# Second head's key weights loaded ahead of the pool's, and token block 2 turned ahead of the value projection, in a two-layer decoder trunk

## The chip, the cores and the metric

The kernel runs on one core of a Trainium2 chip. The metric is the device time of one execution in microseconds (us). The kernel before was timed three times: 1939.69, 1940.29 and 1944.26 us, so its median is 1940.29 us. One more execution was taken with the hardware profiler: it took 1946.18 us in all, of which the traced span, from the first to the last instruction, is 1944.4 us. "Line" numbers such as L276 are lines of the kernel before.

## What is computed

A decoder trunk of two layers over 512 tokens of width 1024, in float32. Cut to its frame, the reference is

```python
for i in range(DEPTH):                     # DEPTH = 2, a = (2 * DEPTH) ** 0.25
    x = layer_norm(a * x + 0.5 * swiglu_ffn(x, ffn_w_in[i, 0], ffn_w_out[i, 0]), ...)
    if m == 0:                             # layer 0
        h = diff_attention(x, da_w_qkv[j], da_w_o[j], da_lam_q[j], da_lam_k[j], ...)
    elif m == 1:                           # layer 1
        h = pool_mixer(x, pool_w[j], pool_b[j], pool_scale[j])
    x = layer_norm(a * x + h, ...)
    x = layer_norm(a * x + memory_cross_attention(x, mem, xa_wq[i], xa_wkv[i], xa_wo[i]), ...)
    x = layer_norm(a * x + 0.5 * swiglu_ffn(x, ffn_w_in[i, 1], ffn_w_out[i, 1]), ...)
```

Two places matter here. In `diff_attention` the rows of x are projected to values, queries and keys, and two softmaxes of each head are combined with a scalar lambda, which is computed from `da_lam_q` and `da_lam_k` (products, sums, two exponentials). In `pool_mixer` x is averaged over four causal windows, a small matrix per group of columns is applied, and a bias and a scale follow. The cross attention behind it needs keys and values of 256 memory rows, `mem @ xa_wkv`, for four heads; they don't depend on x.

## The kernel before, in words

**Numbers.** Every float32 operand of a matmul is split into a high part, which ScalarE (ACT) writes as a rounded copy, and a low part, which VectorE (DVE) writes as the difference (`split`, L116 to L121). A product is three matmuls, high by high, high by low and low by high (`mm3`, L200 to L207). So each block of weights costs one ACT copy and one DVE subtraction before TensorE (PE) can use it.

**Layout.** The 512 tokens are four blocks of 128 rows, `self.X[0]` to `self.X[3]`, which stay in SBUF. For a projection the rows have to lie across: `turn` (L460 to L471) transposes eight 128 by 128 squares of one block on PE into two banks of PSUM and splits them into `xh` and `xl`. `self.late` lists the blocks that are normalised and not yet turned, and `turn_late(wait)` (L448) turns all of them from position `wait` on. `self.turned` holds the last pair of split instructions.

**Order.** Each engine works through its own list of instructions strictly in order. The lists are made at compile time: a scheduler takes the instructions by their place in the program and by when its own model finds them ready, so an instruction that is ready early may be listed ahead of one that stands earlier in the program. `tc.issue_after(i)` lists what is traced in its block behind `i` if both are on one engine; it adds no wait for `i` to finish and no instruction. DMAs of weights are issued from SyncE's queue (SP), in order as well: one that waits for its buffer holds back all behind it. `weave` (L209) interleaves two generators, one that feeds PE steadily and one at its side, by a fixed budget of nanoseconds.

**Where layer 0's attention begins.** The first FFN ends with the layer norm of the four blocks (`summed`, L440, `ln_token`, L363); blocks 0 and 1 are turned while it still runs (L443, L444), blocks 2 and 3 are left in `self.late`. `diff_attention` (L1180) first calls `lam` (L988): two small loads, a product and a sum on DVE, an exponential on ACT, two tiny steps on DVE. Then `da_main` (L1130) projects the values of the first two heads (`da_values`, L1004): blocks 0 and 1 first, then `turn_late()` turns blocks 2 and 3, then blocks 2 and 3. Queries and keys follow head by head. Their weights are split by `cols_rope` (L268 to L277): one ACT copy (L274) and two DVE subtractions (L276).

**Where layer 1's mixer begins.** `mixer` (L1528) traces, in this order: the transposes and splits of the memory rows (`load_memory`), the loads of head 0's key and value weights of the cross attention (`raws`, L1545), the pool's loads (`pool_loads`, L1206: five DMAs, 2 MB, L1211, L1217, L1218), and the splits of x that the pool needs (L1248). Then `weave` runs `early_kv` (L1402), which computes keys and values of heads 0 and 1 through `xa_kv` (L1330), with `pool_mixer` (L1238) at its side. There are two buffers for raw weights of 1 MB, so head 1's key weights can be loaded only when head 0's are split. The pool side has eight steps with band matmuls (L1261 to L1271), each split into `pooled`; behind the second of them stands `pool_weights` (L1221), which scales the pool's matrix and bias on DVE (L1227, L1236). After the eighth the pool's matrix is split, `begin_ln` loads the rows of the norm's gain and bias (`load_row`, L336), and per block two sums (L1282 to L1294) and `ln_token` follow.

Of the kernel before, what the change touches and what calls it, by code (L numbers as in the profile page):

```python
# [9 lines left out]
F32 = mybir.dt.float32  # L10
# [8 lines left out]
D = 1024  # L19
S = 512  # L20
# [79 lines left out]
def drain(units):  # L100
    for _ in units:
        pass
# [7 lines left out]
class Trunk:  # L110
# [74 lines left out]
    def mm(self, name):  # L185
        return self.mmp.tile([P, S], F32, tag="mm", name=name)
# [42 lines left out]

    def raw_cols(self, w, c0, width=256):  # L230
        raw = self.raw_tile((8, 256))
        self.nc.sync.dma_start(
            raw[:, :, :width], w[:, c0 : c0 + width].rearrange("(k p) n -> p k n", p=P)
        )
        return raw
# [29 lines left out]
            self.nc.sync.dma_start(raw[:, j], w[:, c : c + P].rearrange("(k p) n -> p k n", p=P))  # L265
        return raw

    def cols_rope(self, raw, j):  # L268

        nc = self.nc  # L270
        w = self.hl([P, 8, P])
        src = raw[:, j].rearrange("p k (m h q e) -> p (k m) q h e", m=2, h=2, q=2)
        hi, lo = (t.rearrange("p k (m q h e) -> p (k m) q h e", m=2, q=2, h=2) for t in w)
        nc.scalar.copy(hi, src)  # L274
        for q in range(2):
            nc.vector.tensor_sub(lo[:, :, q], src[:, :, q], hi[:, :, q].bitcast(F32))  # L276
        return w  # L277

    def wide(self, raw):
# [198 lines left out]
    def behind(self):  # L478

        return self.tc.issue_after(self.last_mm.ins)  # L480

    def transpose4(self, pt, blocks):
        for j, b in enumerate(blocks):
            self.nc.tensor.transpose(pt[:, j], b, self.ident)
# [645 lines left out]
    def da_main(self):  # L1130

        w, w_o = self.a["da_w_qkv"][0], self.a["da_w_o"][0]
        for n in range(0, DA_H, 2):
            vs = []
            if n < V_FIRST:
                yield from self.da_values(n, vs)
            rq, rk = self.raw_heads(w, n * P), self.raw_heads(w, D + n * P)
            for h in range(n, n + 2):
                q = self.mm("q")
                yield from self.project(q, self.cols_rope(rq, h % 2))  # L1140
                q = self.da_query(q)
                k = self.mm("k")
                yield from self.project(k, self.cols_rope(rk, h % 2))
                k = self.da_key(k)
                sm = self.small("sd", (P, NT, 2))
                self.heads.append((self.clock, {"h": h, "q": q, "k": k, "v": vs, "sm": sm}))
            if not vs:
                yield from self.da_values(n, vs)
        yield from self.to_tokens(self.oT[:4], w_o, 0, 4, True, False, ALPHA)
# [28 lines left out]
                yield W_E[1]  # L1178

    def diff_attention(self, layer, ln):  # L1180
        self.nlam = self.lam()
        self.low_keys = [self.pair("low") for i in range(2)]
        for pair in self.low_keys:
            for m, t in enumerate(pair):
                self.nc.gpsimd.memset(t[HALVES[1 - m]].bitcast(F32), 0.0)
        self.heads, self.oT = [], [None] * DA_H
        self.weave(self.da_main(), self.da_side(), GAP)
        self.begin_ln(layer, ln, 1.0)
        home = lambda tag: lambda: self.pair(tag)
        homes = [[home("qk")] * 4, [home("low"), home("low"), home("p"), home("p")]]  # L1190
        drain(self.to_tokens(self.oT[4:], self.a["da_w_o"][0], 4, 4, False, True, ALPHA, homes))
# [46 lines left out]
    def pool_mixer(self, layer, ln):  # L1238
        nc = self.nc
        bandh, bandf, bandl = self.bandh, self.bandf, self.bandl  # L1240

        self.new_xt()
        xs = [[], []]
        for t in range(NT):
            for half in range(2):
                j = 2 * (t % 2) + half
                x = self.xh[t // 2][:, j], self.xl[t // 2][:, j]
                self.split(x[0], x[1], self.X[t][:, half * S : (half + 1) * S])  # L1248
                xs[half].append(x)
        pooled = []  # L1250
        mm = nc.tensor.matmul
        yield
        for c in range(KC):
            if c == 2:
                with self.tc.issue_after(split[1].ins):
                    self.pool_weights()
            g = c // 2
            half, o = c // 4, slice((c % 4) * P, (c % 4 + 1) * P)
            pp = self.aux("pp")
            with self.behind():  # L1260
                for t in range(NT):  # L1261
                    xh, xl = (x[:, o] for x in xs[half][t])
                    n = BAND if t < NT - 1 else P
                    out = pp[:, t * P : t * P + n]
                    m = (bandf if t == 0 else bandh)[:, g, :n]

                    mm(out, xh, m, start=t == 0, stop=False, skip_group_check=True)
                    if t == 0:
                        m0 = bandl[:, g]
                        mm(out[:, :16], xh, m0, start=False, stop=False, skip_group_check=True)  # L1270
                    mm(out, xl, m, start=False, stop=t == NT - 1, skip_group_check=True)  # L1271
            q = self.pair("pooled")
            split = self.split(q[0], q[1], pp)
            pooled.append(q)
            yield
        wg = self.wide(self.pool_w)
        self.begin_ln(layer, ln, 1.0)
        for t in range(NT):
            o = slice(t * P, (t + 1) * P)
            for half in range(2):  # L1280
                ps = self.aux("ps")
                mm(ps, self.ones, self.pool_b[half], start=True, stop=False)  # L1282
                for j in range(2):
                    g = half * 2 + j
                    for k in range(2):
                        q = pooled[2 * g + k]
                        self.mm3(
                            ps[:, j * 256 : (j + 1) * 256],
                            (q[0][:, o], q[1][:, o]),
                            wg[2 * g + k],  # L1290
                            False,
                            k == 1 and j == 1,
                        )
                self.ln_add(t, half, ALPHA, ps)  # L1294
                yield
            self.turn_late()
            self.ln_token(t)
# [29 lines left out]
        if tag and LINE < 480:  # L1327
            self.stage["mem"].tile([P, (480 - LINE) // 4], F32, name="mempad")

    def xa_kv(self, w, h, raws=None):  # L1330
        nc = self.nc
        rk = raws[0] if raws else self.raw_cols(w, h * 256)
        ps = self.mm("pk").rearrange("p (c n) -> p c n", c=2)
        for j in range(2):
            wk = self.cols(rk, j)
            for k in range(KC):
                yield self.mm3(
                    ps[:, j], (wk[0][:, k], wk[1][:, k]), self.memT[k], k == 0, k == KC - 1
                )
        kv = lambda: tuple(  # L1340
            self.kvp.tile([P, 2, MEM], F32R, tag="kv", name="kv", bufs=8) for _ in range(2)
        )
        kt = kv()
        self.turn_late()
        self.split(kt[0], kt[1], ps)
        wv = self.wide(raws[1] if raws else self.raw_cols(w, D + h * 256))
        ps = self.mm("pv").rearrange("p (m n) -> p m n", m=2)
        for m in range(2):
            o = slice(m * P, (m + 1) * P)
            for k in range(KC):  # L1350
                mt = self.memT[k]
                yield self.mm3(ps[:, m], (mt[0][:, o], mt[1][:, o]), wv[k], k == 0, k == KC - 1)
        v = kv()
        self.split(v[0], v[1], ps)
        return kt, v
# [44 lines left out]
            yield  # L1400

    def early_kv(self, layer, heads, raws):  # L1402
        for h in range(heads):
            self.kv.append((yield from self.xa_kv(self.a["xa_wkv"][layer], h, raws)))
            raws = None

    def xa_main(self, layer):
        wq, wkv = self.a["xa_wq"][layer], self.a["xa_wkv"][layer]
# [119 lines left out]
    def mixer(self, layer, ln):  # L1528
# [5 lines left out]
        else:  # L1534
# [5 lines left out]
            with self.phase_pool(("pooled", "pooled"), "sq", **bufs):  # L1540
                side = self.pool_mixer(layer, ln)
                with self.tc.high_priority():
                    self.load_memory()
                w = self.a["xa_wkv"][layer]
                raws = [self.raw_cols(w, c) for c in (0, D)]  # L1545
                self.pool_loads()
                next(side)
                self.kv = []
                self.weave(self.early_kv(layer, 2, raws), side, 640, 8500)
# [48 lines left out]
```

## Time and profile before

| what | before |
|---|---|
| median of the timed runs | 1940.29 us (1939.69 to 1944.26) |
| profiled execution, in all | 1946.18 us |
| its traced span | 1944.4 us |
| busy: PE / DVE / ACT / GpSimd (POOL) | 99% / 81% / 53% / 15% of the span |
| mean granted clock of PE | 0.994 |
| moved by DMA | 277.96 MB, 143 GB/s on average |

How to read it: PE is busy nearly all the time, so what can be won is PE's idle time, what lies between its matmuls, or time in which PE's clock is not granted in full. The other engines matter where PE waits for one of them. In a timeline a row gives the start, the duration, the engine, the line, the operation, output and inputs, shapes, how many instructions were merged (x4), and in square brackets how long the engine had been idle before and whose end released it. A row of the stretches gives the length, then the busy time of PE, PE's weight loads, DVE, ACT and POOL with the number of instructions, PE's granted clock (1.00 is full), the share of the DMA engines and GB/s.

### The profile page before, as it was taken

The page shows a single profiled execution, that of the slowest core. Times are in us where ns is not written, and L with a number is a line of the kernel's source. Part 1 is how long each engine was busy: PE and PEld are TensorE (multiplying, and loading weights), DVE is VectorE, ACT ScalarE, POOL GpSimd, SP SyncE. Part 2 cuts the span into 40 slices and gives each one's busy share as a digit, 9 for nine tenths or more (in the row PEclk, how much of TensorE's full clock was granted, in tenths as well). Part 3 has the DMA queues.
Part 4 walks back from the last instruction along what each step waited for, and adds up shares of the span by engine and source line. Part 5 has one row for each costly group of instructions (what it writes and reads, how often), then busy time and mean ns, then how long its engine had stood idle before and what let it go on. Part 6 is the DMA issues. An engine that isn't in the chain of part 4 may idle for free.

```text
span 1944.4 us, 32555 instructions
## 1 busy us (share of the span) xinstructions
PE 1916.4 (99%) x13122; PEld 1753.2 (90%) x13122; DVE 1565.4 (81%) x2212; ACT 1025.2 (53%) x1582; POOL 300.3 (15%) x269
## 2 busy tenths in 40 slices
PE   8999999999999999999999999999999999999998
PEld 8999998888778888999998999999898889999997
DVE  7888889888867558889888888898777568988886
ACT  6555454567655435655554655555445336555553
POOL 2112121111110001221220311212000013111210
PEclk9999999999999999999999999999979999999999
DMA  9978772322134317977785687878243347867861
GB/s 240 216 167 181 174 137 77 90 78 75 52 112 141 109 66 194 175 177 163 143 193 170 114 179 163 183 166 173 78 152 131 102 131 134 175 163 170 184 132 60
DMA packets 247031, 277.96 MB, mean 143 GB/s; under 512 B 8288, under 2 KB 212576, under 8 KB 246880
## 3 DMA queue, kind: packets, MB, share of 16 engines
q0 software_dynamic: 92928, 92.29, 30.9%
q1 hardware_dynamic: 153952, 183.59, 28.9%
q8 instruction: 103, 1.69, 0.3%
q14 instruction: 48, 0.39, 0.1%
HBM read 273.75 MB, written 2.10 MB: 142 GB/s over the span
## 4 chain that ended last, share of the span: by engine, by line
PE 80%; DVE 10%; issue 4%; ACT 3%; DMA 2%; POOL 1%; SPq 1%; DVEq 0%; POOLq 0%; ACTq 0%
PE x L204 7%; PE x L205 7%; PE x L206 7%; PE z L205 4%; PE z L204 4%; PE z L206 4%; PE ps L204 3%; PE ps L206 3%; PE ps L205 3%; PE px L204 2%; PE px L206 2%; PE px L205 2%; DVE wl L120 2%; PE y L206 2%; PE x L676 2%
## 5 line engine op out<-in xcount | busy, mean ns | idle before, releaser
L661 POOL DMA_DIRECT2D ra<-in_ffn_w_in_dram x132 | 170.2, 1306 | 1001.0 <-DVE wl L120 966.6
L119 ACT CAST wh<-ra 128x1024 fp32r<-128x1024 f32 x184 | 193.5, 1053 | 218.0 <-PE x L205 72.6
L120 DVE TENSOR_TENSOR wl<-ra,wh 128x1024 fp32r<-128x1024 f32 x184 | 224.0, 1220 | 71.4 <-ACT wh L119 70.8
L119 ACT CAST wh<-rc 128x1024 fp32r<-128x1024 f32 x136 | 143.2, 1053 | 122.0 <-PE x L205 42.0
L204 PE MATMUL x<-xe,wh 128*128 128x256 f32 x704 | 195.5, 278 | 0.0
L205 PE MATMUL x<-xe,wh 128*128 128x256 f32 x704 | 195.3, 277 | 0.0
L206 PE MATMUL x<-xe,wl 128*128 128x256 f32 x704 | 195.2, 277 | 0.0
L119 ACT CAST wh<-b 128x1024 fp32r<-128x1024 f32 x112 | 117.8, 1052 | 134.5 <-PE x L205 68.4
L120 DVE TENSOR_TENSOR wl<-rc,wh 128x1024 fp32r<-128x1024 f32 x136 | 164.7, 1219 | 29.4 <-ACT wh L119 29.0
L120 DVE TENSOR_TENSOR wl<-b,wh 128x1024 fp32r<-128x1024 f32 x112 | 136.7, 1221 | 41.0 <-ACT wh L119 41.0
L204 PE MATMUL x<-xh,wh 128*128 128x256 f32 x544 | 151.4, 278 | 0.0
L205 PE MATMUL x<-xl,wh 128*128 128x256 f32 x544 | 150.9, 277 | 0.0
L206 PE MATMUL x<-xh,wl 128*128 128x256 f32 x544 | 150.9, 277 | 0.0
L205 PEld LDWEIGHTS x<-xe,wh 128*128 128x128 f32 x704 | 132.7, 188 | 1.4
L204 PEld LDWEIGHTS x<-xe,wh 128*128 128x128 f32 x704 | 132.3, 188 | 1.3
L206 PEld LDWEIGHTS x<-xe,wl 128*128 128x128 f32 x704 | 132.2, 188 | 0.0
L120 DVE TENSOR_TENSOR wl<-raw,wh 128x1024 fp32r<-128x1024 f32 x64 | 80.5, 1265 | 56.4 <-ACT wh L119 55.7
L205 PEld LDWEIGHTS x<-xl,wh 128*128 128x128 f32 x544 | 102.6, 189 | 0.7
L204 PEld LDWEIGHTS x<-xh,wh 128*128 128x128 f32 x544 | 102.2, 188 | 0.7
L206 PEld LDWEIGHTS x<-xh,wl 128*128 128x128 f32 x544 | 102.2, 188 | 0.0
L119 ACT CAST wh<-raw 128x1024 fp32r<-128x1024 f32 x64 | 66.5, 1049 | 64.9 <-PE xq L205 21.3
L206 PE MATMUL y<-xh,wl 128*128 128x256 f32 x352 | 98.6, 280 | 1.5 <-DVE wl L120 0.3
(436 smaller groups left out, 6337.1 us busy)
## 6 DMA issues: line engine op xcount, KB each, us to landing
ra<-in_ffn_w_in_dram POOLq DMA_DIRECT2D x132, 512.0 KB, 6.8
rc<-in_ffn_w_in_dram SPq DMA_DIRECT2D x88, 512.0 KB, 5.9
b<-in_ffn_w_out_dram SPq DMA_DIRECT2D x76, 512.0 KB, 4.6
ra<-in_ffn_w_in_dram SPq DMA_DIRECT2D x44, 512.0 KB, 4.6
rc<-in_ffn_w_in_dram POOLq DMA_DIRECT2D x44, 512.0 KB, 7.7
raw<-in_xa_wkv_dram SPq DMA_DIRECT2D x16, 1024.0 KB, 5.4
raw<-in_da_w_qkv_dram SPq DMA_DIRECT2D x16, 512.0 KB, 5.1
raw<-in_xa_wq_dram SPq DMA_DIRECT2D x8, 1024.0 KB, 4.9
```

The costliest lines, as they stand in the source:

```text
L119: self.nc.scalar.copy(hi, src),
L120: self.nc.vector.tensor_sub(lo, src, hi.bitcast(F32)),
L204: mm(out, w[0], x[0], start=start, stop=False, skip_group_check=again)
L205: mm(out, w[0], x[1], start=False, stop=False, skip_group_check=again)
L206: self.last_mm = mm(out, w[1], x[0], start=False, stop=stop, skip_group_check=again)
L661: nc.gpsimd.dma_start(t, source(*block), accum_op=ALU.add)
L676: self.last_mm = nc.tensor.matmul(ps[:, j], v[i][:, k, j * P : (j + 1) * P], x[l][:, k], start=n == i == l == 0, stop=n == 7 and i == 1, s ...
```

## The change

Four edits. In `da_main` block 2 is turned before the value projection, so that only block 3 is left for the middle of it. The low parts of head 0's query and key weights are listed on DVE behind the last split of a turned block. `lam` is traced in head 0, its DVE part behind those low parts. In the mixer, head 1's key weights are loaded as soon as head 0's second block of key weights is split, the pool's five loads are listed behind that load on SP, and the splits of head 1's key weights are listed behind the last splits of x.

```diff
     def raw_cols(self, w, c0, width=256):
         raw = self.raw_tile((8, 256))
-        self.nc.sync.dma_start(
+        self.last_load = self.nc.sync.dma_start(
...
-    def cols_rope(self, raw, j):
+    def cols_rope(self, raw, j, wait=False):
...
         nc.scalar.copy(hi, src)
-        for q in range(2):
-            nc.vector.tensor_sub(lo[:, :, q], src[:, :, q], hi[:, :, q].bitcast(F32))
+        with self.tc.issue_after(self.turned[1].ins) if wait else nullcontext():
+            for q in range(2):
+                self.last_low = nc.vector.tensor_sub(
+                    lo[:, :, q], src[:, :, q], hi[:, :, q].bitcast(F32)
+                )
         return w
...
+    @contextmanager
+    def after(self, group):
+
+        with ExitStack() as ctx:
+            for i in group:
+                ctx.enter_context(self.tc.issue_after(i.ins))
+            yield
...
     def da_main(self):
         w, w_o = self.a["da_w_qkv"][0], self.a["da_w_o"][0]
+        self.turn_late(1)
         for n in range(0, DA_H, 2):
...
                 q = self.mm("q")
-                yield from self.project(q, self.cols_rope(rq, h % 2))
+                ws = self.cols_rope(rq, h % 2, h == 0)
+                yield from self.project(q, ws)
                 q = self.da_query(q)
                 k = self.mm("k")
-                yield from self.project(k, self.cols_rope(rk, h % 2))
+                ws = self.cols_rope(rk, h % 2, h == 0)
+                if h == 0:
+                    with self.tc.issue_after(self.last_low.ins):
+                        self.nlam = self.lam()
+                yield from self.project(k, ws)
...
     def diff_attention(self, layer, ln):
-        self.nlam = self.lam()
...
-                self.split(x[0], x[1], self.X[t][:, half * S : (half + 1) * S])
+                self.x_split = self.split(x[0], x[1], self.X[t][:, half * S : (half + 1) * S])
...
-    def xa_kv(self, w, h, raws=None):
+    def xa_kv(self, w, h, raws=(None, None), then=None):
         nc = self.nc
-        rk = raws[0] if raws else self.raw_cols(w, h * 256)
+        rk = raws[0] or self.raw_cols(w, h * 256)
         ps = self.mm("pk").rearrange("p (c n) -> p c n", c=2)
         for j in range(2):
-            wk = self.cols(rk, j)
+            with self.after(self.x_split if raws[0] and not then else ()):
+                wk = self.cols(rk, j)
+            if then and j == 1:
+                then()
...
-        wv = self.wide(raws[1] if raws else self.raw_cols(w, D + h * 256))
+        wv = self.wide(raws[1] or self.raw_cols(w, D + h * 256))
...
     def early_kv(self, layer, heads, raws):
+        w, keys = self.a["xa_wkv"][layer], {}
+
+        def load_more():
+            keys[1] = self.raw_cols(w, 256)
+            with self.tc.issue_after(self.last_load.ins):
+                self.pool_loads()
+
         for h in range(heads):
-            self.kv.append((yield from self.xa_kv(self.a["xa_wkv"][layer], h, raws)))
-            raws = None
+            then = load_more if h == 0 else None
+            raws = raws if h == 0 else [keys[h], None]
+            self.kv.append((yield from self.xa_kv(w, h, raws, then)))
...
                 raws = [self.raw_cols(w, c) for c in (0, D)]
-                self.pool_loads()
                 next(side)
```

## The prediction

> **What bounds the kernel now.** I read the page first: busy times, the slices with PE's clock, the chain that ended last.
>
> ```profile
> PE 1916.4 (99%) x13122; PEld 1753.2 (90%) x13122; DVE 1565.4 (81%) x2212; ACT 1025.2 (53%) x1582; POOL 300.3 (15%) x269
> ...
> PEclk9999999999999999999999999999979999999999
> PE 80%; DVE 10%; issue 4%; ACT 3%; DMA 2%; POOL 1%; SPq 1%; DVEq 0%; POOLq 0%; ACTq 0%
> ```
>
> PE is the bound, with 28 us of idle in 1944. One slice of 40, from about 1410 to 1458 us, was not granted the full clock. I then cut the two places of the diff into stretches: the start of layer 0's attention (346 to 352 us) and the start of layer 1's mixer (1412 to 1448 us).
>
> ```profile
> 346.00:352.00 6.00, 4.16 (x31) 3.33 (x30) 6.00 (x12) 4.36 (x8) 0.00 (x0) 1.00 0.15 33
> 1412.00:1424.00 12.00, 12.00 (x104) 11.97 (x103) 9.27 (x13) 4.91 (x8) 1.35 (x1) 1.00 0.98 317
> 1424.00:1428.00 4.00, 2.75 (x22) 2.34 (x21) 2.02 (x2) 3.10 (x5) 0.00 (x0) 1.00 0.29 94
> 1428.00:1448.00 20.00, 20.00 (x95) 19.90 (x95) 15.60 (x22) 10.23 (x15) 0.00 (x0) 0.50 0.37 116
> ```
>
> Three prices stand here. **A**: PE idles 6.00 - 4.16 = 1.84 us in the first stretch. **B1**: it idles 4.00 - 2.75 = 1.25 us in the third. **B2**: right behind B1 the clock is 0.50 for 20 us, in which PE counts as busy but gets through 95 matmuls, 4.75 a us, against 104 in 12 us, 8.67 a us, with much the same mixture. That is 20 x (1 - 4.75 / 8.67) = 9.0 us lost. "Busy 99%" hides the largest of the three.
>
> **Edit 1, block 2 turned first, lambda and low parts behind (A).** The timeline of PE, then of ACT, then of DVE:
>
> ```profile
> 346.18 1.97 PE L484 MATMUL pt<-ident,X 128*128 128x128 f32 x16
> 349.01 0.38 PE L204 MATMUL v<-wh,xh 128*128 128x256 f32 x1 [0.86 <-ACT xh L119]
> 349.23 0.28 PE L205 MATMUL v<-wl,xh 128*128 128x256 f32 x1
> 349.98 0.50 PE L204 MATMUL q<-xh,wh 128*128 128x512 f32 x1 [0.47 <-ACT xh L119]
> 350.98 0.38 PE L206 MATMUL v<-wh,xl 128*128 128x256 f32 x1 [0.51 <-DVE xl L120]
> ```
> ```profile
> 346.99 1.28 ACT L998 ACT_TABLE_LOAD   x1
> ...
> 348.39 2.02 ACT L119 CAST xh<-pt 128x512 fp32r<-128x512 f32 x4
> ```
> ```profile
> 335.14 1.28 DVE L383 SCALAR_TENSOR_TENSOR X<-X,rstd,sr 128x1024 f32<-128x1024 f32 x1 [0.44 <-POOL rstd L379]
> ...
> 340.42 0.68 DVE L276 TENSOR_TENSOR wl<-raw,wh 128x512 fp32r<-128x512 f32 x1
> 341.02 0.68 DVE L359 SCALAR_TENSOR_TENSOR X<-X,ps 128x512 f32<-128x512 f32 x1
> ...
> 345.72 1.28 DVE L383 SCALAR_TENSOR_TENSOR X<-X,rstd,sr 128x1024 f32<-128x1024 f32 x1
> ```
>
> PE turns blocks 2 and 3 together (16 transposes at 346.18) and then has nothing but the values of these two blocks, whose splits are late: ACT first loads a table for lambda's exponential (1.28 us), DVE first subtracts weights of queries and keys (L276, the first of them at 340.42). Block 2 was normalised at 335.14 + 1.28 = 336.42, ten us before it is turned. After the change its eight transposes (half of 1.97, so 0.99) stand ahead of the values of blocks 0 and 1, its splits run beside those 48 matmuls (0.115 each, by the 104 in 12 us), and behind them PE turns block 3 alone at 346.18 + 0.99 = 347.2. Block 3 is normalised at 345.72 + 1.28 = 347.0 now; the L276 ahead of its last sum (L359) goes, 0.6, and at most block 2's two subtractions come in, taken at L276's 0.68 each for the same shape, so it is there between 346.4 and 348.4, at the worst 1.2 us late. While it is split (ACT 1.01, half of 2.02, then DVE's last 0.68), PE has block 2's 24 value matmuls, 2.8 us: covered. Nothing is removed: the transposes, splits, lambda's five instructions with their table load and two DMAs all stay; on SP the two lambda loads now come behind head 0's key weights, which gain by that. The low parts of the first query weights come from about 350 on, and PE wants them behind the values of blocks 2 and 3, at 348.2 + 48 x 0.115 = 353.7; what is queued behind them on DVE, the splits of the values, is wanted later still. The table load falls there too, behind copies that are needed sooner. So the three waits go: **1.8 us**, bounded by 0.6 (block 3 late by the 1.2 above) and 1.84. What is late next here: block 3.
>
> **Edit 2, head 1's keys ahead of the pool's loads (B).** SP's queue, then ACT, DVE and PE in that place:
>
> ```profile
> 1410.86 0.34 SPq L1217 DMA_DIRECT2D ps<-in_pool_scale_dram  x1
> ...
> 1413.83 3.38 SPq L232 DMA_DIRECT2D raw<-in_xa_wkv_dram  x2
> ```
> ```profile
> raw<-in_xa_wkv_dram SPq DMA_DIRECT2D x16, 1024.0 KB, 5.4
> ```
> ```profile
> 1424.90 1.99 ACT L119 CAST wh<-raw 128x1024 fp32r<-128x1024 f32 x2 [3.68 <-DMA raw<-in_xa_wkv_dram]
> ```
> ```profile
> 1412.58 1.22 DVE L120 TENSOR_TENSOR wl<-raw,wh 128x1024 fp32r<-128x1024 f32 x1
> ...
> 1425.98 2.36 DVE L120 TENSOR_TENSOR wl<-raw,wh 128x1024 fp32r<-128x1024 f32 x2 [3.96 <-ACT wh L119]
> 1428.26 1.28 DVE L120 TENSOR_TENSOR pooled<-pp,pooled 128x512 fp32r<-128x512 f32 x2
> ```
> ```profile
> 1424.83 0.27 PE L1271 MATMUL pp<-bandh,xl 128*128 128x128 f32 x1
> ```
>
> The keys are issued at 1413.83, the moment the buffer is free (the subtraction of 1412.58 ends at 1413.8): the change does not move this. But five pool loads of 2 MB, issued since 1410.86, are in flight, and the keys land only when ACT starts at 1424.90, 11.1 us later, against a median of 5.4 us for such loads. ACT stood 3.68 us, DVE behind it 3.96, and then PE. With the pool's loads behind them I take the median, by the nearest rows: landing at 1419.2, bounded by 1424.9 (no gain). The splits, behind those of x, then run in the time that ACT and DVE stood: DVE's 2.36 us from 1425.98 - 3.96 on, done at about 1424.4, before the last band matmul of that place ends (1425.1) and PE's waits begin. **B1 goes, and with it what came ahead of the halved clock.** The pool's loads pay: issued from about 1414.3 on, 3.4 us later; at the worst 11.1 us again for the last one, 1427.7. Their first reader is L1227, below; the cover is about gone at that end, 0.5 us.
>
> **But PE's 10.3 us (1.25 + 9.0) is not all won: the norm behind it is late next.**
>
> ```profile
> 1443.18 1.42 SPq L336 DMA_DIRECT2D pooled<-in_ln_g_dram  x2
> 1444.65 0.96 SPq L336 DMA_DIRECT2D pooled<-in_ln_b_dram  x2
> ```
> ```profile
> pooled<-in_ln_b_dram SPq DMA_DIRECT2D x2, 256.0 KB, 6.5
> ```
> ```profile
> 1430.06 0.68 DVE L1227 TENSOR_TENSOR ps<-ps 128x512 f32<-128x512 f32 x1
> ...
> 1441.53 1.21 DVE L120 TENSOR_TENSOR wl<-raw,wh 128x1024 fp32r<-128x1024 f32 x1
> ...
> 1455.02 1.41 DVE L383 SCALAR_TENSOR_TENSOR X<-X,rstd,pooled 128x512 f32<-128x512 f32 x2
> ```
>
> Gain and bias of the norm are queued on SP behind a load that waits for the last subtraction of head 1's values (1441.53, ends 1442.7). The last is issued at about 1445.1 and lands 6.5 later, 1451.6; its reader starts at 1455.02, so there are 3.4 us of slack. DVE fixes when this queue moves, and DVE moves by less than PE: its second `pooled` can't start before the band matmul ending at 1425.1 and ACT's copy (0.5), 1425.6 instead of 1428.9, so all behind it moves by 3.2 to 3.3. I take 3.2 (bounds 0 and its idle 3.96). The norm's chain can then move by 3.2 + 3.4 = 6.6 us, less than PE's 10.3: **B is 6.6 us**, and 3.7 us of a new PE wait appear where it turns block 0.
>
> **The sum**: 1.8 + 6.6 = 8.4 us. Against the profiled execution's own 1946.18 us that gives 1937.8. The median of the runs shown, 1940.29, lies 5.9 below that execution; carried over, **1931.9 us**, 0.43% less. Behind both places PE's order and work are as before, so I let the gain pass to the end.
>
> [...] The trace: 0.50 followed 1.25 us of idle in 4 and stayed for 20 us of gapless work, while 1.84 us idle in 6 left it at 1.00. [...]
>
> **The rivals.**
> *The whole of PE's loss comes back*: the scheduler lists the gain and bias rows ahead of the waiting load. Then 1.8 + 10.3 = 12.1, 1928.2 us. For: they need nothing that is late. Against: they sit behind it now.
> *The timed runs hardly had the halved clock*: only the profiled one shows clocks, and two timed runs lie 6 us below it. Then the norm's rows bounded there already, and B is DVE's 3.2: 5.0 in all, 1935.3 us. Against: with 9.0 less of PE time the profiled run would lie below every timed one, so the loss was at least partly hidden or shared.
> *The keys land no earlier*, because loads behind them in one queue share the engines: B is nothing, 1938.5 us. For: the load took 11.1 us with 2 MB ahead of it, and as much stands behind it after the change.
> *Slower*: PE's new wait at block 0 of layer 1 has the clock halved, as B1 did: 9.0 us behind 1448 instead of at 1428, where the norm no longer hides any of it. If the timed runs were without B2 and B wins nothing else, 1940.29 - 1.8 + 9.0 = 1947.5 us. It decides from a wait of about B1's size, 1.25 us. For: 3.7 us is longer. Against: A's waits, longer than B1's, left the clock alone.
>
> **How the numbers follow.** Chances: forecast 0.45, whole loss back 0.12, timed runs without the drop 0.22, keys no earlier 0.08, slower 0.13. What this kernel's measurement can tell from no change is about 0.3%, 5.8 us: below 1934.5 is faster (0.45 + 0.12 = 0.57), up to 1946.1 within (0.22 + 0.08 = 0.30), above it slower (0.13). The range from 1927 to 1939 takes in all but the last, with an us at the low end for the bounds of the terms.
>
> **What would show it.** A right: no PE wait above 0.3 us between 340 and 352, transposes as 8 and 8. B right: the head 1 key load lands within 6 us, ACT's wait for it is gone, the clock is 1.00 there, and a wait of the norm for its gain or bias row, some us long, comes in its place. Wrong: a stretch of 0.50 anywhere, `pooled` waiting for `pool_weights`, or new waits in the attention behind 352 because the lists changed.

## The result

Eighteen executions of each kernel: before 1941.96 us median (1938.90 to 1950.20), after 1937.54 us (1934.66 to 1940.91). The ratio is 0.9974, 95% interval 0.9965 to 0.9982, so the change is worth 5.0 us (3.5 to 6.8). The profiled execution of the changed kernel took 1937.88 us in all, 8.3 us less than the profiled one before. So the two ways of comparing disagree, 5.0 against 8.3, and the experiments are about that difference.

The page of the profile after: PE has 9.9 us less of busy time for the same 13122 matmuls, and the slice of PE's clock that showed 7 is gone.

```profile
PE 1906.5 (98%) x13122; PEld 1742.6 (90%) x13122; DVE 1565.3 (81%) x2212; ACT 1025.2 (53%) x1582; POOL 300.7 (16%) x269
...
PEclk9999999999999999999999999999999999999999
PE 80%; DVE 11%; issue 3%; ACT 3%; DMA 2%; POOL 1%; SPq 0%; DVEq 0%; POOLq 0%; ACTq 0%
```

The same stretches as before, in the same columns:

```profile
346.00:352.00 6.00, 6.00 (x54) 6.00 (x53) 4.36 (x7) 2.72 (x5) 0.00 (x0) 1.00 0.12 29
1412.00:1424.00 12.00, 12.00 (x105) 12.00 (x104) 11.06 (x14) 6.30 (x10) 1.35 (x1) 1.00 0.88 284
1424.00:1428.00 4.00, 4.00 (x36) 4.00 (x36) 3.40 (x7) 2.41 (x5) 0.00 (x0) 1.00 1.09 353
1428.00:1448.00 20.00, 17.29 (x141) 16.54 (x140) 16.06 (x25) 10.18 (x16) 0.54 (x1) 1.00 0.41 128
```

A's 1.84 us and B1's 1.25 us of idle are gone. In the last stretch PE gets through 141 matmuls at the full clock where it got through 95 at half; in exchange it now idles 2.71 us there (0.68 for a split of `pooled`, 2.03 for the norm). The timelines of SP, ACT and DVE after the change say why: the keys go out at 1412.72 ahead of the pool's loads, ACT splits them at 1420.02 with no wait for a DMA, and DVE waits for the norm's gain instead. (Lines behind about L300 have moved: L336, L381 and L383 of before are L339, L384 and L386 here.)

```profile
1412.72 0.37 SPq L232 DMA_DIRECT2D raw<-in_xa_wkv_dram  x1
1413.18 0.53 SPq L1227 DMA_DIRECT2D pw<-in_pool_w_dram  x1
...
1438.99 1.05 SPq L339 DMA_DIRECT2D pooled<-in_ln_g_dram  x2
1440.09 1.14 SPq L339 DMA_DIRECT2D pooled<-in_ln_b_dram  x2
```
```profile
1420.02 1.99 ACT L119 CAST wh<-raw 128x1024 fp32r<-128x1024 f32 x2
```
```profile
1445.38 1.41 DVE L384 SCALAR_TENSOR_TENSOR X<-X,mean,pooled 128x512 f32<-128x512 f32 x2 [3.48 <-DMA pooled<-in_ln_g_dram]
```
```profile
1447.65 1.29 PE L495 MATMUL pt<-ident,X 128*128 128x128 f32 x8 [2.03 <-DVE X L386]
```

### The profile page after: what moved, and what is told of

It reads as the page before. It is cut to its first block, busy times and chain, and to the rows that moved or that the text cites. A ratio compares the mean times of both kernels' runs of the same rounds, so it can differ in the third digit from the quotient of the medians.

```text
span 1936.1 us, 32553 instructions
## 1 busy us (share of the span) xinstructions
PE 1906.5 (98%) x13122; PEld 1742.6 (90%) x13122; DVE 1565.3 (81%) x2212; ACT 1025.2 (53%) x1582; POOL 300.7 (16%) x269
## 4 chain that ended last, share of the span: by engine, by line
PE 80%; DVE 11%; issue 3%; ACT 3%; DMA 2%; POOL 1%; SPq 0%; DVEq 0%; POOLq 0%; ACTq 0%
PE x L204 7%; PE x L205 7%; PE x L206 7%; PE z L205 4%; PE z L206 4%; PE z L204 4%; PE ps L204 4%; PE ps L206 4%; PE ps L205 4%; PE px L206 2%; PE px L204 2%; PE px L205 2%; DVE wl L120 2%; PE y L206 2%; PE x L687 2%
## 5 line engine op out<-in xcount | busy, mean ns | idle before, releaser
L204 PE MATMUL z<-xh,wh 128*128 128x256 f32 x352 | 98.3, 279 | 1.4 <-ACT xh L119 1.4
```

The costliest lines, as they stand in the source:

```text
L204: mm(out, w[0], x[0], start=start, stop=False, skip_group_check=again)
```

## The experiments

Theory 1 is the prediction's: B1 brings on the halved clock B2, every execution has both, and the change removes both. Theory 2 is its second rival ("the timed runs hardly had the halved clock"): the halved clock is a thing of the profiled execution, and what other executions gain is smaller. Each timed execution comes with its mean granted clock over the span, so the two can be told apart without a profile: 20 us at half clock in 1944 lower the mean by 0.005.

**The kernel before, once more**, with no edit.

> The kernel before once more, for the granted clock of each timed execution, of which only the profiled one was known (0.994, of which the 20 us at half rate in the mixer are 0.005). If the halved stretch is part of nearly every execution (theory 1), the mean clocks lie near 0.994. If it comes and goes (theory 2), most lie at 0.997 to 0.999, as those of the changed kernel do, and the profiled execution was one of the slower ones; time and mean clock then fall together, by up to 9 us for 0.005.

Ratio 1.0007 (0.9998 to 1.0017), profiled execution 1941.49 us. This is what an ordinary execution of the kernel before looks like; first its stretches, then ACT, DVE and PE:

```profile
346.00:352.00 6.00, 4.23 (x32) 3.48 (x31) 6.00 (x13) 4.77 (x8) 0.00 (x0) 1.00 0.17 45
1424.00:1428.00 4.00, 4.00 (x37) 3.83 (x35) 3.60 (x5) 2.77 (x5) 0.00 (x0) 1.00 0.27 85
1428.00:1448.00 20.00, 18.28 (x149) 17.50 (x148) 16.19 (x26) 11.52 (x18) 0.54 (x1) 1.00 0.44 139
1448.00:1451.00 3.00, 1.06 (x8) 0.67 (x8) 3.00 (x5) 0.20 (x1) 0.00 (x0) 1.00 0.32 120
1451.00:1454.70 3.70, 3.70 (x20) 3.60 (x19) 2.61 (x8) 3.25 (x6) 0.19 (x1) 0.56 0.00 0
```
```profile
1423.32 2.00 ACT L119 CAST wh<-raw 128x1024 fp32r<-128x1024 f32 x2 [2.12 <-DMA raw<-in_xa_wkv_dram]
```
```profile
1447.85 1.42 DVE L381 SCALAR_TENSOR_TENSOR X<-X,mean,pooled 128x512 f32<-128x512 f32 x2 [3.34 <-DMA pooled<-in_ln_g_dram]
```
```profile
1440.09 0.39 PE L206 MATMUL ps<-wh,pooled 128*128 128x256 f32 x1 [0.61 <-DVE pooled L120]
1441.82 0.39 PE L206 MATMUL ps<-wh,pooled 128*128 128x256 f32 x1 [1.11 <-DVE pooled L120]
...
1450.14 1.29 PE L484 MATMUL pt<-ident,X 128*128 128x128 f32 x8 [1.91 <-DVE X L383]
```

A is there (1.77 us), B1 and B2 are not. The keys landed 1.6 us earlier than in the first profile, and ACT was done in time for PE. The DMA view, for this one load, first of the profile before, then of this run, then after the change (last column: us to landing):

```profile
raw<-in_xa_wkv_dram SPq DMA_DIRECT2D x1, 1024.0 KB, 11.1
```
```profile
raw<-in_xa_wkv_dram SPq DMA_DIRECT2D x1, 1024.0 KB, 9.5
```
```profile
raw<-in_xa_wkv_dram SPq DMA_DIRECT2D x1, 1024.0 KB, 5.4
```

And the wait for the norm's gain, which the prediction expected as a new one, stands there already. From 1428 on PE loses 1.72 us in two waits for splits of `pooled`, 1.94 in 1448 to 1451 for the norm and, by the clock of 0.56 behind that, 3.7 x 0.44 = 1.6: 5.3 us in all. Against that stand the 2.71 of the changed kernel: one wait for `pooled` fewer, the same wait for the norm, and no low clock behind it. So in such an execution B wins 2.6 us, not 6.6.

**A alone, B alone.** The first keeps the edits in `da_main`, `cols_rope` and `diff_attention`, the second those in `mixer`, `early_kv` and `xa_kv`.

> The changed kernel with the mixer's part undone: only block 2's early turn, lambda and the first low parts. Theory 1 and 2 alike: the PE waits of 1.84 us between 346 and 352 are gone, 1.8 us less than before (ratio 0.9991). If A's gain is given back in the attention behind it, the time is that of before.

> The changed kernel with the attention's part undone: only head 1's keys ahead of the pool's loads. The keys land within 6 us and the norm waits some 3.5 us for its gain row, as in the changed kernel. Theory 1 (halved clock in nearly every execution of before): 6.6 us less than before (0.9966). Theory 2 (the clock comes and goes): DVE's 3.2 us less (0.9984).

A alone: 0.9982 (0.9974 to 0.9991), 3.5 us. B alone: 0.9987 (0.9979 to 0.9995), 2.5 us. Both are gains, and together they make 6.0 us where the whole change measured 5.0, which the intervals allow. B alone is of theory 2's size (3.2 us), not of theory 1's (6.6). DVE's wait for the gain row is 3.66 us with A alone and 3.12 us with B alone: the norm ends B with or without the change.

**Part of A at a time.** With the early turn alone:

```diff
-                ws = self.cols_rope(rq, h % 2, h == 0)
+                ws = self.cols_rope(rq, h % 2)
...
-                ws = self.cols_rope(rk, h % 2, h == 0)
-                if h == 0:
-                    with self.tc.issue_after(self.last_low.ins):
-                        self.nlam = self.lam()
+                ws = self.cols_rope(rk, h % 2)
...
 def diff_attention(self, layer, ln):
+        self.nlam = self.lam()
```

> The changed kernel, but in layer 0 only the early turn of block 2 stays: lambda and head 0's low parts are listed as in the kernel before. Nothing is computed otherwise. Theory 1 (the early turn is what closes A's waits, because block 2's 24 value matmuls lie over block 3's splits): no PE wait above 0.3 us between 340 and 353, and the time of the changed kernel, 0.997 of before, about 1937.5 us. Theory 2 (lambda's table load and the low parts ahead of the splits make the waits): 0.9 us or more of PE wait stay between 346 and 353, about 0.998, 1938.5 to 1939.5 us.

With the listing alone:

```diff
 def da_main(self):
-        self.turn_late(1)
```

> The changed kernel without the early turn of block 2: blocks 2 and 3 are turned together again, lambda and head 0's low parts are listed late as in the changed kernel. Theory 1 (early turn): PE still waits 1.0 us or more for the splits of 16 squares between 346 and 353, 0.998 of before. Theory 2 (listing): the waits shrink below 0.5 us, 0.997 of before, about 1937.5 us. This kernel and the one with the early turn alone add up to the whole of A only if the two edits do not overlap.

Ratios 0.9973 (0.9963 to 0.9983) and 0.9971 (0.9961 to 0.9982): with either one the time can't be told from that of the whole change. The stretch of A, with the early turn alone and then with the listing alone:

```profile
346.00:352.00 6.00, 5.77 (x50) 5.56 (x50) 5.42 (x12) 4.45 (x8) 0.55 (x1) 1.00 0.24 69
```
```profile
346.00:352.00 6.00, 5.98 (x53) 5.78 (x52) 4.58 (x7) 4.51 (x7) 0.38 (x1) 1.00 0.26 65
```

Both theories said that one edit is the cure and the other does little; neither held. The late splits need two things: 16 squares to split at once, and a table load and weight splits ahead of them (these two were only moved together). Taking away either is enough: PE's idle in this stretch falls from 1.84 us to 0.23 or 0.02.

**The keys' splits not listed behind those of x.**

```diff
-            with self.after(self.x_split if raws[0] and not then else ()):
+            with self.after(()):
```

> The changed kernel without the listing of head 1's key splits behind the last splits of x. Nothing is computed otherwise. Theory 1 (the listing protects the splits of x, which the next band matmuls read, from 4 us of key splits on ACT and DVE): PE waits 1 us or more for xh or xl between 1416 and 1426, 1 to 3 us slower than the changed kernel, about 0.998 of before. Theory 2 (the keys land after the splits of x anyway: these end at about 1420, the keys land at 1418 at the earliest): no new wait, the time of the changed kernel, 0.997.

0.9970 (0.9955 to 0.9984), and PE is busy without a gap from 1412 to 1432. ACT did take the first key split ahead of the last two of x (at 1415.32, behind a 2.06 us wait for the load), but at 1.05 us no PE wait came of it. This edit is worth nothing that can be measured.

**The norm's rows early.** In the changed kernel the rows of gain and bias are loaded right behind the pool's loads:

```diff
     with self.tc.issue_after(self.last_load.ins):
         self.pool_loads()
+        self.wide_gain = False
+        self.early_gb = [
+            self.load_row(tag, self.a[n][layer, 1]) for tag, n in zip(self.gain, ("ln_g", "ln_b"))
+        ]
```

> The changed kernel with the norm's gain and bias rows loaded behind the pool's loads, ahead of the load that waits for head 1's values. If the rows are what is late next, DVE's wait of 3.48 us for them and PE's wait behind it go: up to 3.5 us less than the changed kernel (0.998 of it), 0.9955 of before. If something else is as late, such as DVE's own work ahead of the norm, the time stays. Another 1 MB ahead of head 1's values could make these late instead: their copy now starts at 1432.3, some 4 us behind their landing.

(The norm takes these rows in place of loading its own.) 1934.27 us median, 0.9964 (0.9952 to 0.9976): faster than the kernel before; from the changed kernel (0.9974) the times alone don't separate it, as the intervals overlap. The traces do: DVE no longer waits for the row, and PE has no idle in this stretch:

```profile
1440.96 1.41 DVE L385 SCALAR_TENSOR_TENSOR X<-X,mean,pooled 128x512 f32<-128x512 f32 x2 [0.63 <-ACT sq L381]
```
```profile
1440.00:1448.00 8.00, 8.00 (x69) 7.87 (x68) 7.21 (x16) 4.39 (x9) 1.01 (x2) 1.00 0.21 73
```

The same edit in the kernel before, with the rows' loads traced right behind the pool's:

> The kernel before, with one thing moved: the rows of the norm's gain and bias in layer 1's mixer are loaded right behind the pool's loads and ahead of head 1's keys. Theory 1 (in an ordinary execution these rows set the end of the mixer; the keys' place is worth little by itself): no wait of the norm for its rows, 2.5 to 4 us less than before, 0.998 to 0.9987. Theory 2 (the keys' late landing bounds, through PE): 256 KB more ahead of the keys cost about 1 us, PE waits behind 1424, the time is that of before or above. In the first case the two edits of the mixer together (changed kernel with the rows early: 0.9964) are more than this one alone by what the keys' place gives, about 3 us with A's 3 us taken off 0.9964: near nothing to 1.5 us.

0.9989 (0.9976 to 1.0001), 2.1 us by the middle of the interval, which just reaches no difference. (The scheduler put the rows not ahead of head 1's keys but right behind them, at 1415.04 after 1414.62, so the keys had only the pool's loads ahead of them.) By chance its profiled execution is one with the halved clock. The keys landed 11.3 us after their issue, PE waited, and then:

```profile
1426.00:1428.50 2.50, 0.94 (x6) 0.53 (x5) 1.44 (x2) 2.50 (x4) 0.00 (x0) 1.00 0.95 309
1428.50:1449.00 20.50, 20.50 (x96) 20.40 (x97) 16.28 (x22) 10.83 (x16) 0.00 (x0) 0.50 0.35 111
```

In the first profile the same cut reads:

```profile
1425.50:1428.00 2.50, 1.25 (x9) 1.03 (x9) 2.02 (x2) 2.50 (x5) 0.00 (x0) 1.00 0.07 23
1428.00:1448.50 20.50, 20.50 (x97) 20.40 (x97) 15.60 (x22) 10.23 (x15) 0.00 (x0) 0.50 0.38 117
```

So twice a PE wait for the keys (1.25 and 1.56 us of idle in 2.50), and twice 20.5 us at half clock behind it. It remained to bring the wait about on purpose.

**The keys made late.** First the pool's matrix was loaded twice in `pool_loads`, in the kernel before:

> The kernel before, with the pool's matrix (1 MB) loaded twice in a row into the same buffer, so that head 1's keys are issued and land some 3 to 6 us later. The result is the same. Theory 1 (a wait of PE for these keys is what halves the clock for 20 us behind it): PE waits 3 us or more behind 1424, the clock is 0.50 for about 20 us behind that in most executions, not in 3 of 41, and the time is 6 to 10 us above before, 1.003 to 1.005. Theory 2 (the halved stretch comes by chance, whatever PE waited): PE waits 3 us or more, the clock stays above 0.9 in the profile or drops for a few us only, mean clocks of the timed runs stay at 0.997 to 0.999, and the time is 1 to 4 us above before.

0.9990 (0.9977 to 1.0002), and it is no test of theory 1: the scheduler listed the second load behind the keys (1419.01 against 1413.66 on SP), which landed after 9.7 us as in an ordinary execution. It shows one thing: a third MB behind keys that are on time brings no 20 us at half clock (mean clock 0.997 or 0.998 in all 11). So the keys were listed behind the second load, and in a further kernel, with 3 in place of 2, behind a third:

```diff
+        for _ in range(2):
+            self.held = nc.sync.dma_start(self.pool_w, w.rearrange("(k p) n -> p k n", p=P))
...
+        with self.tc.issue_after(self.held.ins) if self.held and not raws else nullcontext():
+            rk = raws[0] if raws else self.raw_cols(w, h * 256)
```

> The kernel before, with the pool's matrix (1 MB) loaded twice into the same buffer and head 1's keys listed behind the second load, which itself waits for the first to land. The result is the same. The first load was issued at 1411.5 and let the second go at 1419.0 in the run where it stood behind the keys, so the keys are issued at about 1419.5, 5.7 us later than before, and land between 1425 and 1429. Theory 1 (a PE wait of an us or more at this place halves the clock for 20 us): PE waits 1 to 4 us behind 1424 in every execution, the clock is 0.50 for about 20 us behind it, most timed runs have a mean clock of 0.993 or 0.994 (12 of 111 had it so far with the keys behind the pool's loads), median 6 to 10 us above before, 1.003 to 1.005. Theory 2 (the halved stretch comes by chance): mean clocks of 0.997 and more in nearly all runs, 1 to 4 us above before, 1.0005 to 1.002.

> As the kernel with the keys behind two loads of the pool's matrix, but behind three: the keys are issued at about 1425 and land at 1430 or later, so PE waits some 5 to 7 us, with no matmul for most of it. The result is the same. Theory 1 (the halved stretch follows the wait, whatever its length above an us): 20 us at 0.50 in most executions, and 4 to 6 us more than with two loads, by the longer wait alone: 1.006 to 1.008. Theory 2 (by chance): 0.997 and more, 5 to 8 us above before. A third (the halved stretch needs a gap of a few us without any matmul): with two loads the clock stays, here it is halved.

1.0035 (1.0021 to 1.0048) and 1.0062 (1.0049 to 1.0075). All 6 executions with two loads have a mean clock of 0.992 or 0.993, all 5 with three of 0.991 or 0.992. PE's timeline and the stretch at half clock, with two loads and then with three:

```profile
1434.12 0.58 PE L204 MATMUL pk<-mem0h,wh 128*128 128x256 f32 x1 [3.37 <-ACT wh L119]
```
```profile
1432.40:1456.30 23.90, 21.71 (x99) 21.33 (x100) 17.12 (x22) 12.69 (x18) 0.00 (x0) 0.50 0.43 133
1456.50:1460.00 3.50, 3.50 (x31) 3.45 (x30) 0.93 (x3) 0.00 (x0) 0.00 (x0) 1.00 0.60 215
```
```profile
1434.73 0.58 PE L204 MATMUL pk<-mem0h,wh 128*128 128x256 f32 x1 [9.36 <-ACT wh L119]
```
```profile
1428.20:1459.00 30.80, 23.80 (x109) 23.41 (x110) 15.69 (x20) 11.25 (x16) 0.00 (x0) 0.50 0.59 190
```

Theory 1 is right about the cause: a PE wait for these keys is followed by the halved clock, in all four profiles that have one (1.25 us or more) and, by their mean clock, in the nine other executions of these two kernels. That it takes a gap of some us without any matmul is not so: in the first profile two waits of 0.49 and 0.76 us within 2.50 came ahead of 20.5 us at 0.50. Three loads cost 5.2 us more than two (1.0062 less 1.0035) for 6.0 us more of wait.

**How often it happens by itself.** Beside the experiments and as one of them the kernel before ran 99 times; 14 of these have a mean clock of 0.994 or less, at 1944.3 to 1950.7 us, on average 4.9 us above the median of their set. That these are executions with the 20 us is read from the clock: no trace of the 14 was kept, and the two traces with the long stretch have 0.994 and 0.993. Of the other kernels with the keys behind the pool's loads and not held back, 2 of 35 executions are that low (A alone 0 of 12, the rows early 2 of 12, the pool's matrix twice 0 of 11). Of 70 executions of the kernels with the keys ahead (the changed kernel, B alone, the two parts of A with B, the two with the rows early, the one without the listing), none is below 0.996. Theory 2 is right about the share: about one execution in seven of the kernel before.

**What each place is worth in the traces.** GpSimd's `rstd` (one per block and norm) marks the time. From the start of block 3's ahead of the mixer to the start of block 3's behind it the profiles have (the two kernels with the keys held back left out):

| keys and rows | profiles | us |
|---|---|---|
| keys behind the pool's loads, late, halved clock | kernel before, the same with the rows early | 57.5, 58.3 |
| keys behind the pool's loads, on time | kernel before again, A alone, the pool's matrix twice | 52.7, 53.4, 52.4 |
| keys ahead | changed, B alone, the two parts of A with B, without the listing behind x | 49.8 to 50.2 |
| keys ahead, rows early | with all of the change, with the fewest edits | 47.6, 47.4 |

So the keys' place wins 2.2 to 3.6 us in an ordinary execution and 7.3 to 8.5 in one with the halved clock, and the rows 2.3 to 2.8 more. For A the time from block 2's `rstd` ahead of the attention to the first one behind it is 244.9 to 247.9 us in the seven profiles with A as before (mean 246.1), and 243.9 to 244.4 in the seven with both edits of A or one (mean 244.0): 2.0 us.

**The fewest edits.** Last, the kernel with the rows early, less the early turn and less the listing behind x:

> The kernel with the rows of the norm's gain and bias loaded early, less two edits of the change that by themselves were worth nothing measurable: the early turn of block 2, and the listing of head 1's key splits behind those of x. Nothing is computed otherwise. Theory 1 (each of the two has a cover: lambda and the low parts listed late, and keys that land after the splits of x): 0.9955 to 0.9975 of before, as with them (0.9964). Theory 2 (they are needed together): 1 us or more of PE wait between 346 and 353 or between 1416 and 1426, 0.998.

1934.61 us median, 0.9962 (0.9947 to 0.9977), as with them.

## Why the prediction was right or wrong

- **The number**: 1931.9 us forecast, 1937.54 measured. By the medians the change wins 4.4 us where 8.4 were forecast; the remaining 1.7 us of the miss are the kernel before, whose 18 executions have a median of 1941.96 where the first three had 1940.29. The range of 1927 to 1939 holds the measured time because it was drawn to take in three of the rivals as well, and 0.57 of the chances stood on a time below 1934.5. That is the width of the range, not the forecast's mechanism.
- **A, 1.8 us**: its mechanism holds. After the change there is no PE wait between 340 and 352, the transposes come block by block: block 2's as 4 and 4 at 341.37 and 342.29, block 3's 8 at 347.73 (predicted 347.2). A alone measured 3.5 us (1.7 to 5.0); 1.8 is at the edge of that. The six other profiles with A as before have 1.34 to 2.51 us of idle in this stretch, and the 2.0 us by `rstd` above agree. They lie within the interval, so nothing here shows more than that. That edit 1 is a turn and a listing together was too much: each covers the waits alone.
- **The keys**: forecast to land in 5.4 us, landed in 5.4. The rival that loads behind them would hold them back is dead: 5.3 to 5.5 us in the five profiles with the pool's loads behind in which this load's landing was read (changed, B alone, the early turn alone, the rows early, without the listing behind x). These paid nothing: their first reader starts on DVE at 1425.86 without a wait for a DMA. (The cover of 0.5 us doesn't come out of the prediction's own rows: its worst case, 1427.7, lies 0.8 behind that reader's 1430.06 less the shift of 3.2.)
- **"B1 goes, and with it what came ahead of the halved clock"**: right, and shown from both sides. In the first profile PE idled 1.25 us within 2.50 and the clock fell to 0.50 for 20.5 us; with the keys held back PE waited 3.37 and 9.36 us, and it was 0.50 for 23.9 and 30.8. In the changed kernel that idle is gone (PE is busy for 4.00 us of 4.00 from 1424 on), and the clock is 1.00 from 1424 to 1448.
- **The norm late next**: right in kind and nearly in size. DVE waits 3.48 us for the gain row; PE's wait at block 0 is 2.03 us, not 3.7. It is not new, though: an ordinary execution of the kernel before has it as well (3.34 us on DVE, 1.91 on PE), which the sum for B left out. Loading the rows early removes it.
- **The sum against the profiled execution**: 8.4 forecast, 1946.18 to 1937.8; measured 1937.88. Between the norm ahead of the mixer and the one behind it 7.3 us arise (57.5 less 50.2), where B had 6.6, and ahead of it block 3's `rstd` is 1.1 us earlier (1416.28 for 1417.38), where A had 1.8. So the agreement to 0.1 us is luck in part: two misses of 0.7 cancel.
- **The step that failed** is the last one: "The median of the runs shown, 1940.29, lies 5.9 below that execution; carried over, 1931.9 us". Some 5 of those 5.9 us were the halved clock itself. Six of seven executions don't have it, so what the change wins by removing it can't be taken off their median. They gain A's 1.8 us and B's 2.6, 4.4 as the medians do; the ratio gains a little from the rare ones besides (an estimate: 4.9 in one of seven, 0.7). The second rival (5.0 us, 1935.3, chance 0.22) had the right reason and, by the ratio, the right gain; its B of 3.2 measured 2.5 alone. The argument held against it, that the loss was at least partly hidden, was true, and no argument: the norm hides some 5 of the 10.3 us, and the other 5 are just what sets the profiled execution apart from the median.
- **The slower rival**: the wait at block 0 was to halve the clock for 20 us. In the profiled ordinary execution of the kernel before that wait is there already (1.91 us), and the clock behind it is 0.56 for 3.7 us, worth 1.6. In the changed kernel it stays at 1.00 behind its 2.03 us. Each of the three profiles with the keys behind the pool's loads and on time has one such short stretch: 1451.4 to 1454.8 (kernel before again), 1448.8 to 1452.2 (A alone) and, there ahead of that wait, 1443.1 to 1446.5 (the pool's matrix twice). In the four with the keys ahead whose clock was read there (changed, the rows early, without the listing, the fewest edits) it is 1.00 from 1440 to 1456.
- **The whole of PE's loss back** (12.1 us): the rows early do open the queue, but the 9.0 in it was in one execution of seven, so this gives 7 us.

## What to carry to other kernels

Before a gain read from one profiled execution is taken off the median, see whether the profiled execution shares the median's loss: if it is slower by some us, and the loss to be removed is of that size, it may be an event of that execution alone, as here; for a loss by the clock the mean clock of each timed run tells. A load that usually lands just in time is worth moving even if the median hardly shows it: it takes away the executions in which it is late. And where two causes must meet for a wait, as A's, one edit can be enough; try each alone before keeping both.

## What the runs showed of the hardware

- The clock fell 1.7 to 2.9 us after PE's first idle moment at this place (four profiles), and came back after 20.5, 20.5, 23.9 and 30.8 us, the last two in the kernels with the keys held back, where PE's longest wait was 3.37 and 9.36 us. In both of 20.5 us PE worked without a gap (20.50 us busy). Four other stretches at half clock, in layer 0's attention or in this mixer, lasted about 3.4 us each: the three short ones above, of which that from 1451.4 on came behind 1.94 us of idle, and one with two loads between 352 and 360 us (a clock of 0.79 over these 8 us, which is 3.4 at half). Why this place has the long kind stays open, and so does why A's waits were followed by a short one in that profile (1.34 us of idle in six) and by neither in others: with 1.77 to 1.84 us of idle the clock is 1.00 from 352 to 358 (kernel before, before again, B alone), with 2.51 it is 1.00 up to 354, as far as it was read there (kernel before, rows early). It was not tried.
- The same 1 MB load behind the same 2 MB took 9.5, 9.7, 9.7, 11.1 and 11.3 us in five profiles, 5.3 to 5.5 in the five named above with the 2 MB behind it. An us and a half lies between the three without the 20.5 us at half clock (9.5 to 9.7 us, mean clock 0.998) and the two with it (11.1 and 11.3 us, 0.994 and 0.993).
